# A hybrid SSD and delta-rule layer on one core: the first RMSNorm scaled in place on token rows, its transposes read from PSUM

## The chip, the cores and the metric

The kernel runs on one core of a Trainium2 chip. The time is device microseconds of one execution. A run is one execution; before the change three runs were taken, with a median of 2346.11 us (2344.76 to 2347.41). One more execution was taken by the hardware profiler.

## The reference, cut to what matters

One step of an encoder layer on 336 tokens: 16 learned meta tokens and 256 prompt tokens of one stream, 64 sample tokens of another. `D_MODEL` is 2048. The change lies in the first line of the layer and its first uses:

```python
def _rmsnorm(x, w):
    xf = xf * lax.rsqrt(jnp.mean(xf * xf, axis=-1, keepdims=True) + EPS)
    return (xf * w.astype(jnp.float32)).astype(x.dtype)

u = _rmsnorm(x, norm_mix_w)
z_a, xbc_a, dt_a, qkv_b, z_b, beta_b, a_b, gate_a, gate_b = jnp.split(u @ w_in, SPLIT_IDX, axis=-1)
```

`u @ w_in` feeds a Mamba-2 mixer (causal convolution, chunked scan, gate, norm) and a gated DeltaNet; their outputs go through `w_out`, two sigmoid gates and the residual, then a squared-ReLU MLP, a last residual and a last norm. All is float32.

## The kernel before, in words

**Products.** Every float32 operand of a product is split into a high part of type float32r and a rest (`lo = x - hi`); a product is three matmuls, hi by hi, hi by the rest of the other, rest by hi. Activations lie channel-major: channels on the 128 partitions, the 336 tokens along the free axis. `uh` and `ul` are the two parts of u, 16 tiles of 128 channels each (a *k-tile*).

**Weights.** All weight blocks of the kernel stand in one list (`stream`), 592 pieces of four k-tiles by 256 columns (512 KB). `wload` (line 193) sends piece n through SP's DMA queue into one of three `raw` buffers; `wsplit` (201) lets ScalarE make `hi` and VectorE `lo` (GpSimd for piece 3, line 208). `block` (213) is a generator that runs over the pieces of one block: it loads piece n+3, splits up to piece n+2 (in the first block `hold` keeps it from that, and the start does it by hand), and gives two output tiles `pt` of 128 columns by 336 tokens; each step between two yields is three matmuls.

**The order of the work.** TensorE's instructions keep the order of the program text throughout (line 73). Inside `manual` (343 to 472) all engines and queues do. Outside it, a scheduler places the instructions of the other engines and of the DMA queues by its own estimate of when they are ready; such an instruction may slip in between those of the manual part. `run` (240) weaves the matmuls of a projection with the scan of the group before.

**The start.** x comes as three tiles of 112 token rows: `xs[0]` holds the meta tokens and 96 prompt rows, `xs[1]` 112 prompt rows, `xs[2]` 48 prompt and 64 sample rows. SP's queue carries x0 and x1, then five small loads `prow` (norm weights and convolution biases as rows), then x2, then the first three weight pieces. For each tile `sumsq` (321) forms the sums of squares (ScalarE, VectorE or half by half), `root` (334) the reciprocal root with a power on GpSimd, and `flip` (328) transposes four k-tiles at a time into a PSUM buffer of the pool `scr` (four buffers), from which ScalarE or VectorE copies them to `xT` (16 k-tiles of unscaled x; the residual needs it later, `scratch` writes it to DRAM). The roots stand per token on partitions; to scale channel-major data, `spread_d` (339) puts them on diagonals, a product with ones (`prx`) spreads them over all partitions, and `rbx` is their copy. Then, per k-tile, `u_scale` (380) forms `ut = xT * rbx` on VectorE for even and GpSimd for odd k-tiles, and `u_split` (384) makes `uh` (ScalarE, with the norm weight as scale) and `ul` (VectorE). The loop at 464 emits these four k-tiles ahead of the first block's steps.

**Behind the block.** The last step of the first block is left for `run`. After `manual.close()` come the loads of the convolution weights and states as rows (`cra`, `crb`, `sra`, `srb`, 475 to 486), of `dvec` (488) and `pb` (490 to 493), and of `wt` (503, 504); the rows are turned by TensorE and copied by VectorE (`load_cols`, 306), and `ptok` (505) is the projection of the 64 narrow columns. All these tiles but `dvec` lie in pool `sp`, opened after `xctx.close()` (375), in memory that x held. `tokens` (516) then computes `nega` from `pb` on ScalarE, among others.

Of the kernel before, what the change touches and what calls it, by code (L numbers as in the profile page):

```python
# [21 lines left out]
NT = NMETA + NPR + NSA  # L22
# [20 lines left out]
def tile_hybrid_step(ctx: ExitStack, tc: tile.TileContext, i: dict, o: dict):  # L43
    nc = tc.nc
# [148 lines left out]
    def wload(n):  # L193
        if n >= len(stream) or n in raws:
            return
        raw = wpool.tile([P, 4, 256], F32, tag="raw", name="raw", bufs=3)
        for c0, src in stream[n]:
            nc.sync.dma_start(raw[:, :, c0:c0 + src.shape[1]], src.rearrange("(k p) c -> p k c", p=P))
        raws[n] = raw

    def wsplit(n):
        if n >= len(stream) or n in split:
            return
        wload(n)
        hi = wpool.tile([P, 4, 256], F32R, tag="hi", name="hi", bufs=3)
        act(hi, raws[n])
        lo = wpool.tile([P, 4, 256], F32R, tag="lo", name="lo", bufs=3)
        tt(G if n == 3 else V, lo, raws[n], hi.bitcast(F32), SUB)
        split[n] = hi, lo

    used, hold = [0], [len(stream)]
# [73 lines left out]
        G.memset(t, 0.0)  # L285
    xctx = ExitStack()
    xp = xctx.enter_context(tc.tile_pool(name="xp", bufs=1))
    xs = []
    segs = [[(0, "meta", 0, 16), (16, "pr", 0, 96)], [(0, "pr", 96, 112)], [(0, "pr", 208, 48), (48, "sa", 0, 64)]]
    src = {"meta": i["meta_tokens"], "pr": i["x_prompt"][0], "sa": i["x_sample"][0]}  # L290
    def load_x(n):
        for p0, s, r0, nr in segs[n]:
            nc.sync.dma_start(xs[n][p0:p0 + nr, :], src[s][r0:r0 + nr, :])

    for n in range(3):
        xs.append(xp.tile([112, D], F32, name=f"x{n}"))
# [17 lines left out]
    junk = acc.rearrange("p k n -> p (k n)")[:112, :]
    ssx = sp0.tile([112, 4], F32, name="ssx")
    rsx = sp0.tile([112, 3], F32, name="rsx")
    dgx = sp0.tile([112, 3, 112], F32, name="dgx")
    rbx = sp0.tile([P, NT], F32, name="rbx")
    HD = D // 2

    def sumsq(f, x, d0, n):
        d = junk[:, d0:d0 + x.shape[1]]
        if f is act:
            act(d, x, AF.Square, accum_out=ssx[:, n:n + 1])
        else:
            V.scalar_tensor_tensor(out=d, in0=x, scalar=1.0, in1=x, op0=MUL, op1=MUL, accum_out=ssx[:, n:n + 1])

    def flip(n, k):
        ps = scr("pu").rearrange("p (k t) -> p k t", k=4)[:, :, :112]
        for m in range(4):  # L330
            transp(ps[:, m, :], xs[n][:, (k + m) * P:(k + m + 1) * P])
        return xT[k // 4][:, :, n * 112:(n + 1) * 112], ps

    def root(n):
        r = rsx[:, n:n + 1]
        V.tensor_scalar(out=r, in0=ssx[:, n:n + 1], scalar1=1.0 / D, scalar2=EPS, op0=MUL, op1=ADD)
        tt(G, r, r, nhalf_pow[:112, 0:1], ALU.pow)

    def spread_d(n):
        V.tensor_scalar(out=dgx[:, n, :], in0=ident[:112, :112], scalar1=rsx[:, n:n + 1], scalar2=None, op0=MUL)  # L340

    manual = ExitStack()
    manual.enter_context(tc.manual_schedule())

    pw_ = scr("pwarm")
    for n in range(8):
        mm(pw_[:, :P], ident, ident)
    prx = psb.tile([P, 512], F32, tag="big", name="prx")
    sumsq(act, xs[0], 0, 0)
    for k in range(0, KD, 4):  # L350
        (V.tensor_copy if k < 8 else act)(*flip(0, k))
    root(0)
    sumsq(V, xs[1], D, 1)
    for k in range(0, KD, 4):
        act(*flip(1, k))
    root(1)
    load_cols(par, prow, 73)
    for n in range(3):
        wload(n)
    sumsq(act, xs[2][:, :HD], 0, 2)  # L360
    sumsq(V, xs[2][:, HD:], D, 3)
    tt(V, ssx[:, 2:3], ssx[:, 2:3], ssx[:, 3:4], ADD)
    root(2)
    spread_d(0)
    spread_d(1)
    act(*flip(2, 0))
    late = [flip(2, k) for k in (4, 8, 12)]
    spread_d(2)
    wsplit(0)
    for n in range(3):  # L370
        mm(prx[:, n * 112:(n + 1) * 112], ones[:112, :], dgx[:, n, :])
    act(rbx, prx[:, :NT])
    for a in late:
        act(*a)
    xctx.close()
    sp = start.enter_context(tc.tile_pool(name="sp", bufs=1))

    ut = {}

    def u_scale(k):  # L380
        ut[k] = sp0.tile([P, NT], F32, tag="ut", name="ut", bufs=6)
        tt(G if k % 2 else V, ut[k], xT[k // 4][:, k % 4, :], rbx, MUL)

    def u_split(k):
        t, w = ut.pop(k), par[:, NM + k:NM + k + 1]
        act(uh[:, k, :], t, AF.Copy, scale=w)
        stt(ul[:, k, :], t, w, uh[:, k, :].bitcast(F32), MUL, SUB)

# [68 lines left out]

    main0 = kept(proj_ssd(0), tiles0)  # L460
# [12 lines left out]
    hold[0] = len(stream)

    cra = sp.tile([96, P], F32, name="cra")
    nc.sync.dma_start(cra, i["ssd_conv_w"][0].rearrange("k (t c) -> (k t) c", c=P))
    crb = [sp.tile([96, P], F32, name=f"crb{n}") for n in range(2)]
    crb_src = i["gdn_conv_w"][0].rearrange("k (t c) -> (k t) c", c=P)
    for n in range(2):
        nc.sync.dma_start(crb[n], crb_src[n * 96:(n + 1) * 96, :])  # L480
    sra = sp.tile([72, P], F32, name="sra")
    nc.sync.dma_start(sra, i["state_ssd_conv"][0, 0].rearrange("k (t c) -> (k t) c", c=P))
    srb = [sp.tile([72, P], F32, name=f"srb{n}") for n in range(2)]
    srb_src = i["state_gdn_conv"][0, 0].rearrange("k (t c) -> (k t) c", c=P)
    for n in range(2):
        nc.sync.dma_start(srb[n], srb_src[n * 72:(n + 1) * 72, :])
# [8 lines left out]
    load_cols(cwa.rearrange("p k t -> p (k t)"), cra, 96)  # L495
    load_cols(sta.rearrange("p k t -> p (k t)"), sra, 72)
    for n in range(2):
        load_cols(cwb.rearrange("p k t -> p (k t)")[:, n * 96:(n + 1) * 96], crb[n], 96)
        load_cols(stb.rearrange("p k t -> p (k t)")[:, n * 72:(n + 1) * 72], srb[n], 72)


    wt = sp.tile([P, KD, 64], F32, name="wt")
    nc.sync.dma_start(wt[:, :, 0:32], win[:, C_DT:C_DT + 32].rearrange("(k p) c -> p k c", p=P))
    nc.sync.dma_start(wt[:, :, 32:64], win[:, C_BETA:C_BETA + 32].rearrange("(k p) c -> p k c", p=P))
# [746 lines left out]
```

## Time and profile before

| | us |
|---|---|
| median of three runs | 2346.11 |
| profiled execution | 2343.37 |
| its span from first to last instruction | 2341.5 |
| TensorE busy (matmul) | 2300.9 |
| VectorE busy | 1354.5 |
| ScalarE busy | 1065.4 |
| GpSimd busy | 333.1 |

Times in the profile are microseconds from the start of the span. PE is TensorE's matmul, PEld its weight load, DVE VectorE, ACT ScalarE, POOL GpSimd, SPq the issue of DMAs by SyncE. "L61" is line 61 of the kernel, mostly that of a helper (58 matmul, 61 activation, 64 tensor_tensor, 67 scalar_tensor_tensor, 87 transpose, 309 copy of turned rows). A tile is named without its buffer number. The granted clock (PEclk) is the share of TensorE's full clock.

### The profile page before, as it was taken

The page shows a single profiled execution, that of the slowest core. Times are in us where ns is not written, and L with a number is a line of the kernel's source. Part 1 is how long each engine was busy: PE and PEld are TensorE (multiplying, and loading weights), DVE is VectorE, ACT ScalarE, POOL GpSimd, SP SyncE. Part 2 cuts the span into 40 slices and gives each one's busy share as a digit, 9 for nine tenths or more (in the row PEclk, how much of TensorE's full clock was granted, in tenths as well). Part 3 has the DMA queues.
Part 4 walks back from the last instruction along what each step waited for, and adds up shares of the span by engine and source line. Part 5 has one row for each costly group of instructions (what it writes and reads, how often), then busy time and mean ns, then how long its engine had stood idle before and what let it go on. Part 6 is the DMA issues. An engine that isn't in the chain of part 4 may idle for free.

```text
span 2341.5 us, 40643 instructions
## 1 busy us (share of the span) xinstructions
PE 2300.9 (98%) x16393; PEld 2278.7 (97%) x16393; DVE 1354.5 (58%) x2147; ACT 1065.4 (46%) x1830; POOL 333.1 (14%) x488
## 2 busy tenths in 40 slices
PE   7999999999999999999999999999999999999997
PEld 6999999999999999999999999999999999999997
DVE  6675757575765547668668567444444444444444
ACT  5664545455445545554554445433343244234433
POOL 3142414141121112112212110000000000000000
PEclk9999999999999999999999999999999999999999
DMA  7845454546565555645556644544544454445543
GB/s 193 224 131 161 136 174 126 173 124 179 157 199 172 151 163 137 163 147 144 144 149 161 171 142 145 151 150 151 148 152 153 146 152 153 146 152 151 166 143 117
DMA packets 411046, 362.87 MB, mean 155 GB/s; under 512 B 48329, under 2 KB 407834, under 8 KB 410394
## 3 DMA queue, kind: packets, MB, share of 16 engines
q1 hardware_dynamic: 410746, 360.15, 52.8%
q8 instruction: 128, 2.10, 0.4%
q14 instruction: 60, 0.49, 0.1%
q10 hardware_dynamic: 112, 0.13, 0.0%
HBM read 340.57 MB, written 19.66 MB: 154 GB/s over the span
## 4 chain that ended last, share of the span: by engine, by line
PE 90%; DVE 5%; DMA 2%; ACT 1%; issue 1%; SPq 1%; POOL 0%; ACTq 0%; DVEq 0%
PE pbig L58 84%; DVE lo L64 1%; DMA raw<-in_w_in_dram 1%; PE po L58 1%; DVE pr L64 1%; DVE ubt L858 1%; PE pS L58 0%; DVE c L67 0%; PE pyd L58 0%; PE pw L58 0%; PE pkk L58 0%; PE pqk L58 0%; ACT hi L61 0%; PE ph L58 0%; DMA x<-in_x_sample_dram 0%
## 5 line engine op out<-in xcount | busy, mean ns | idle before, releaser
L64 DVE TENSOR_TENSOR lo<-raw,hi 128x1024 fp32r<-128x1024 f32 x591 | 738.2, 1250 | 711.2 <-ACT hi L61 705.1
L61 ACT ACTIVATE hi<-raw 128x1024 fp32r<-128x1024 f32 x592 | 627.5, 1060 | 890.4 <-PE pbig L58 840.1
L58 PE MATMUL pbig<-uh,hi 128*128 128x320 f32 (+2 forms) x2176 | 689.2, 317 | 4.2 <-ACT uh L61 4.2
L58 PE MATMUL pbig<-ul,hi 128*128 128x320 f32 (+2 forms) x2176 | 682.5, 314 | 4.0 <-DVE ul L67 3.9
L58 PE MATMUL pbig<-uh,lo 128*128 128x320 f32 (+2 forms) x2176 | 681.0, 313 | 0.7 <-DVE lo L64 0.7
L58 PEld LDWEIGHTS pbig<-uh,hi 128*128 128x128 f32 x2176 | 411.3, 189 | 10.0 <-ACT uh L61 4.7
L58 PEld LDWEIGHTS pbig<-ul,hi 128*128 128x128 f32 x2176 | 411.5, 189 | 6.0 <-DVE ul L67 5.8
L58 PEld LDWEIGHTS pbig<-uh,lo 128*128 128x128 f32 x2176 | 411.4, 189 | 1.0 <-DVE lo L64 1.0
L58 PE MATMUL pbig<-hh,hi 128*128 128x320 f32 x1024 | 318.0, 311 | 0.0
L58 PE MATMUL pbig<-hnl,hi 128*128 128x320 f32 x1024 | 317.1, 310 | 0.0
L58 PE MATMUL pbig<-hl,hi 128*128 128x320 f32 x1024 | 316.2, 309 | 0.0
L58 PE MATMUL pbig<-hh,lo 128*128 128x320 f32 x1024 | 316.2, 309 | 0.0
L58 PE MATMUL pbig<-hnh,lo 128*128 128x320 f32 x1024 | 315.8, 308 | 0.0
L58 PE MATMUL pbig<-hnh,hi 128*128 128x320 f32 x1024 | 315.1, 308 | 0.0
L58 PEld LDWEIGHTS pbig<-hnh,lo 128*128 128x128 f32 x1024 | 192.9, 188 | 0.0
L58 PEld LDWEIGHTS pbig<-hl,hi 128*128 128x128 f32 x1024 | 192.6, 188 | 0.0
L58 PEld LDWEIGHTS pbig<-hh,hi 128*128 128x128 f32 x1024 | 192.6, 188 | 0.0
L58 PEld LDWEIGHTS pbig<-hnh,hi 128*128 128x128 f32 x1024 | 192.3, 188 | 0.2
L58 PEld LDWEIGHTS pbig<-hh,lo 128*128 128x128 f32 x1024 | 192.5, 188 | 0.0
L58 PEld LDWEIGHTS pbig<-hnl,hi 128*128 128x128 f32 x1024 | 192.2, 188 | 0.0
L58 PE MATMUL pbig<-yh,hi 128*128 128x320 f32 x512 | 161.2, 315 | 1.1 <-ACT yh L61 1.1
L58 PE MATMUL pbig<-yl,hi 128*128 128x320 f32 x512 | 157.6, 308 | 0.3 <-DVE yl L64 0.3
(303 smaller groups left out, 2418.4 us busy)
## 6 DMA issues: line engine op xcount, KB each, us to landing
raw<-in_w_in_dram SPq DMA_DIRECT2D x256, 512.0 KB, 3.9
raw<-in_w_up_dram SPq DMA_DIRECT2D x128, 512.0 KB, 3.9
raw<-in_w_down_dram SPq DMA_DIRECT2D x128, 512.0 KB, 3.5
raw<-in_w_out_dram SPq DMA_DIRECT2D x64, 512.0 KB, 3.4
raw<-in_w_in_dram SPq DMA_DIRECT2D x32, 256.0 KB, 3.5
em<-rowd SPq DMA_DIRECT2D x8, 512.0 KB, 5.8
u<-uD SPq DMA_DIRECT2D x4, 768.0 KB, 5.5
eab<-rowd SPq DMA_DIRECT2D x8, 336.0 KB
```

Of the source, the lines that this page charges most:

```text
L58: nc.tensor.matmul(out, lhsT=lhsT, rhs=rhs, start=start, stop=stop, **kw)
L61: nc.scalar.activation(out=out, in_=in_, func=func, **kw)
L64: eng.tensor_tensor(out=out, in0=a, in1=b, op=op)
L858: V.tensor_reduce(out=ubt[:NE, j0:, s], in_=v, axis=AX.X, op=ADD)
```

## The change

x is loaded first on SP's queue and `prow` through ScalarE's. The first three weight pieces follow x, then the row loads of the convolution parameters and `wt`, both now in pool `sp0`. After a tile's root is known and its unscaled transposes are taken, `scale` multiplies the token rows in place (ScalarE, VectorE or half by half). `u_tile` then transposes one k-tile of all three tiles into one PSUM buffer, from which `uh` and `ul` are made; three k-tiles are emitted ahead of the block's steps. `warmer` puts matmuls of the identity between. `spread_d`, `prx`, `rbx`, `u_scale` and `ut` go, and piece 3's `lo` is VectorE's. `xctx` closes after the block. The diff, cut to its core:

```diff
-        tt(G if n == 3 else V, lo, raws[n], hi.bitcast(F32), SUB)
+        tt(V, lo, raws[n], hi.bitcast(F32), SUB)
...
-    load_x(0)
-    load_x(1)
+    manual = ExitStack()
+    manual.enter_context(tc.manual_schedule())
+    warm = sp0.tile([P, 1], F32, name="warm")
+    act(warm, ones[:, 0:1], AF.Square)
     prow = sp0.tile([73, P], F32, name="prow")
     for r0, name, nr in ((NM, "norm_mix_w", 16), (SN, "ssd_norm_w", 16), (NP_, "norm_mlp_w", 16), (CB_, "ssd_conv_b", 24), (GN, "gdn_norm_w", 1)):
-        nc.sync.dma_start(prow[r0:r0 + nr, :], i[name][0].rearrange("(t c) -> t c", c=P))
-    load_x(2)
+        nc.scalar.dma_start(prow[r0:r0 + nr, :], i[name][0].rearrange("(t c) -> t c", c=P))
+    for n in range(3):
+        load_x(n)
+    for n in range(3):
+        wload(n)
+
+    turned = []
+    for dst, source, n in ((cwa, i["ssd_conv_w"][0], 96), (sta, i["state_ssd_conv"][0, 0], 72), (cwb, i["gdn_conv_w"][0], 96), (stb, i["state_gdn_conv"][0, 0], 72)):
+        flat = source.rearrange("k (t c) -> (k t) c", c=P)
+        cols = dst.rearrange("p k t -> p (k t)")
+        for r0 in range(0, flat.shape[0], n):
+            row = sp0.tile([96, P], F32, name=f"row{len(turned)}")
+            nc.sync.dma_start(row[:n, :], flat[r0:r0 + n, :])
+            turned.append((cols[:, r0:r0 + n], row, n))
+    wt = sp0.tile([P, KD, 64], F32, name="wt")
+    nc.sync.dma_start(wt[:, :, 0:32], win[:, C_DT:C_DT + 32].rearrange("(k p) c -> p k c", p=P))
+    nc.sync.dma_start(wt[:, :, 32:64], win[:, C_BETA:C_BETA + 32].rearrange("(k p) c -> p k c", p=P))
...
+    def warmer(n):
+        ps = scr("pwarm")
+        for _ in range(n):
+            mm(ps[:, :P], ident, ident)
...
+    def scale(f, n, c0, c1):
+        x, r = xs[n][:, c0:c1], rsx[:, n:n + 1]
+        if f is act:
+            act(x, x, AF.Copy, scale=r)
+        else:
+            V.tensor_scalar(out=x, in0=x, scalar1=r, scalar2=None, op0=MUL)
+
+    def u_tile(k):
+        ps = scr("pu")
+        for n in range(3):
+            transp(ps[:, n * XW:(n + 1) * XW], xs[n][:, k * P:(k + 1) * P])
+        w = par[:, NM + k:NM + k + 1]
+        act(uh[:, k, :], ps[:, :NT], AF.Copy, scale=w)
+        stt(ul[:, k, :], ps[:, :NT], w, uh[:, k, :].bitcast(F32), MUL, SUB)
...
     main0 = kept(proj_ssd(0), tiles0)
     hold[0] = 0
-    for k in range(4):
-        u_scale(k)
+    cp = V.tensor_copy
+    warmer(10)
+    load_cols(par, prow, 73)
+    sumsq(act, xs[0], 0, 0)
+    for k in range(0, KD, 4):
+        flip(0, k, cp if k < 8 else act)
+    root(0)
+    warmer(4)
+    scale(act, 0, 0, D)
+    sumsq(V, xs[1], D, 1)
+    for k in range(0, KD, 4):
+        flip(1, k, act)
+    root(1)
+    warmer(4)
+    scale(V, 1, 0, HD)
+    scale(act, 1, HD, D)
+    sumsq(act, xs[2][:, :HD], 0, 2)
+    sumsq(V, xs[2][:, HD:], D, 3)
+    tt(V, ssx[:, 2:3], ssx[:, 2:3], ssx[:, 3:4], ADD)
+    root(2)
+    for k in range(0, KD, 4):
+        flip(2, k, act)
+    warmer(2)
+    for c in range(2):
+        scale(V, 2, c * 512, (c + 1) * 512)
+    scale(act, 2, HD, D)
+    wsplit(0)
+    LEAD = 3
+    for k in range(LEAD):
+        u_tile(k)
     for k in range(KD):
-        u_split(k)
-        if k + 4 < KD:
-            u_scale(k + 4)
-        if k % 4 == 1 and k < KD - 4:
-            wsplit(k // 4 + 1)
+        if k + LEAD < KD:
+            u_tile(k + LEAD)
         for _ in range(2 if k < KD - 1 else 1):
             next(main0)
+        if k % 4 == 0 and k < KD - 4:
+            wsplit(k // 4 + 1)
     manual.close()
+    xctx.close()
+    sp = start.enter_context(tc.tile_pool(name="sp", bufs=1))
...
+    for t in turned:
+        load_cols(*t)
```

## Rows read from the trace of the kernel before

**Rows 1.** Engine windows: start:end, length, busy us of each engine (instructions), PEclk, DMA share, GB/s

```profile
160.00:2341.50 2181.50, 2158.30 (x15462) 2140.30 (x15460) 1249.01 (x1960) 972.72 (x1677) 285.55 (x406) 1.00 0.52 153
```

**Rows 2.** Timeline of TensorE's matmuls: start, length, instruction, idle time before and what ended it

```profile
21.36 0.42 PE L58 MATMUL pbig<-uh,hi 128*128 128x336 f32 x1 [2.30 <-ACT uh L61]
...
23.11 0.48 PE L58 MATMUL pbig<-uh,lo 128*128 128x336 f32 x1
...
23.39 0.48 PE L58 MATMUL pbig<-ul,hi 128*128 128x336 f32 x1
...
48.40 0.40 PE L58 MATMUL ptok<-uh,wtr 128*128 128x336 f32 x1
...
53.42 0.32 PE L58 MATMUL pbig<-uh,hi 128*128 128x336 f32 x1
```

**Rows 3.** TensorE's waits from 20 to 48.4 us: total us, times, longest

```profile
PE pbig L58 <- ACT uh L61: 4.2, 2, 2.3
PE pbig L58 <- DVE ul L67: 3.9, 4, 2.1
PE pcol L87 <- DVE cwa L309: 1.0, 1, 1.0
```

**Rows 4.** Engine windows inside the start, columns as in rows 1

```profile
18.70:21.36 2.66, 0.36 (x4) 0.18 (x3) 1.71 (x4) 2.27 (x6) 1.74 (x2) 1.00 0.08 1
21.36:25.70 4.34, 3.89 (x14) 3.55 (x14) 4.34 (x5) 4.16 (x7) 3.42 (x3) 0.61 0.26 73
...
42.80:46.00 3.20, 3.20 (x13) 3.20 (x13) 0.81 (x3) 0.08 (x2) 0.00 (x0) 0.50 1.31 181
...
29.00:36.00 7.00, 4.48 (x26) 3.68 (x25) 7.00 (x8) 2.79 (x5) 5.38 (x3) 1.00 0.06 1
```

**Rows 5.** Groups by form on VectorE, 0 to 60 us: count, busy us, mean ns

```profile
L67 DVE SCALAR_TENSOR_TENSOR ul<-ut,par,uh 128x336 fp32r<-128x336 f32 x16 | 12.3, 798 | 3.0 <-ACT uh L61 2.8
...
L64 DVE TENSOR_TENSOR lo<-raw,hi 128x1024 fp32r<-128x1024 f32 x6 | 7.3, 1219 | 3.3 <-ACT hi L61 3.3
```

**Rows 6.** Timeline inside the first block: VectorE, GpSimd, ScalarE and SP

```profile
26.54 1.04 DVE L67 SCALAR_TENSOR_TENSOR ul<-ut,par,uh 128x336 fp32r<-128x336 f32 x2
26.56 0.61 SPq L488 DMA_DIRECT2D dvec<-in_ssd_d_dram  x1
...
33.58 2.61 POOL L64 TENSOR_TENSOR lo<-raw,hi 128x1024 fp32r<-128x1024 f32 x1
...
33.91 3.13 DVE L67 SCALAR_TENSOR_TENSOR ul<-ut,par,uh 128x336 fp32r<-128x336 f32 x2
...
40.76 0.24 ACT L61 ACTIVATE nega<-pb 128x48 f32<-128x48 f32 x1 [7.81 <-DMA pb<-in_gdn_a_log_dram]
```

**Rows 7.** The chain that ended last, at its start: start us, length, what

```profile
1.26 5.52 DMA x<-in_x_prompt_dram
...
6.79 8.07 DMA x<-in_x_sample_dram
```

**Rows 8.** Timeline of x's transposes, copies and Square

```profile
6.91 1.73 PE L87 MATMUL pu<-ident,x 112*128 112x112 f32 x16 [1.64 <-DMA x<-in_x_prompt_dram]
...
10.72 1.85 ACT L61 ACTIVATE xT<-pu 128x448 f32<-128x448 f32 x4 [0.85 <-PE pu L87]
...
14.97 1.06 ACT L61 ACTIVATE acc<-x 112x1024 f32<-112x1024 f32 x1 [2.40 <-DMA x<-in_x_sample_dram]
...
15.01 2.96 PE L87 MATMUL pu<-ident,x 112*128 112x112 f32 x16 [3.03 <-DMA x<-in_x_sample_dram]
```

**Rows 9.** A scaling of 1024 columns on ScalarE, by form, from 2325 us on

```profile
L61 ACT ACTIVATE yt<-yt,frs 128x1024 f32<-128x1024 f32 x2 | 2.2, 1142 | 0.2 <-POOL frs L64 0.2
```

**Rows 10.** Groups by form on ScalarE, 0 to 60 us

```profile
L61 ACT ACTIVATE uh<-ut,par 128x336 fp32r<-128x336 f32 x16 | 8.1, 574 | 3.3 <-DVE ut L64 3.3
L61 ACT ACTIVATE hi<-raw 128x1024 fp32r<-128x1024 f32 x7 | 7.4, 1055 | 0.0
```

**Rows 11.** DMA issues, 0 to 90 us: count, KB each, median us to landing

```profile
wt<-in_w_in_dram SPq DMA_DIRECT2D x2, 256.0 KB, 5.8
```

More of the change, by code (lines that the diff above doesn't have):

```diff
@@ L287, in tile_hybrid_step @@
     xp = xctx.enter_context(tc.tile_pool(name="xp", bufs=1))
-    xs = []
+    XW = NT // 3
     segs = [[(0, "meta", 0, 16), (16, "pr", 0, 96)], [(0, "pr", 96, 112)], [(0, "pr", 208, 48), (48, "sa", 0, 64)]]
     src = {"meta": i["meta_tokens"], "pr": i["x_prompt"][0], "sa": i["x_sample"][0]}
+    xs = [xp.tile([XW, D], F32, name=f"x{n}") for n in range(3)]
+    HD = D // 2
     def load_x(n):
@@ L293, in load_x @@
             nc.sync.dma_start(xs[n][p0:p0 + nr, :], src[s][r0:r0 + nr, :])
-    for n in range(3):
-        xs.append(xp.tile([112, D], F32, name=f"x{n}"))
-    load_x(0)
-    load_x(1)
+    manual = ExitStack()
+    manual.enter_context(tc.manual_schedule())
+    warm = sp0.tile([P, 1], F32, name="warm")
+    act(warm, ones[:, 0:1], AF.Square)
     prow = sp0.tile([73, P], F32, name="prow")
     for r0, name, nr in ((NM, "norm_mix_w", 16), (SN, "ssd_norm_w", 16), (NP_, "norm_mlp_w", 16), (CB_, "ssd_conv_b", 24), (GN, "gdn_norm_w", 1)):
-        nc.sync.dma_start(prow[r0:r0 + nr, :], i[name][0].rearrange("(t c) -> t c", c=P))
-    load_x(2)
-    warm = sp0.tile([P, 1], F32, name="warm")
-    act(warm, ones[:, 0:1], AF.Square)
+        nc.scalar.dma_start(prow[r0:r0 + nr, :], i[name][0].rearrange("(t c) -> t c", c=P))
[14 more added lines that the diff above has]
+    nc.sync.dma_start(wt[:, :, 32:64], win[:, C_BETA:C_BETA + 32].rearrange("(k p) c -> p k c", p=P))
     def load_cols(dst, row, n):
@@ L309, in load_cols @@
         V.tensor_copy(dst, ps[:, :n])
+    def warmer(n):
+        ps = scr("pwarm")
+        for _ in range(n):
+            mm(ps[:, :P], ident, ident)
     xT = [cpool.tile([P, 4, NT], F32, tag=t, name="xT", bufs=b) for t, b in (("q", 2), ("k", 2), ("v", 1))]
     xT.append(sp0.tile([P, 4, NT], F32, name="xT3"))
[L314 to L319, printed above, removed]
+    junk = acc.rearrange("p k n -> p (k n)")[:XW, :]
+    ssx = sp0.tile([XW, 4], F32, name="ssx")
+    rsx = sp0.tile([XW, 3], F32, name="rsx")
     def sumsq(f, x, d0, n):
@@ L326, in sumsq, with flip @@
             V.scalar_tensor_tensor(out=d, in0=x, scalar=1.0, in1=x, op0=MUL, op1=MUL, accum_out=ssx[:, n:n + 1])
-    def flip(n, k):
-        ps = scr("pu").rearrange("p (k t) -> p k t", k=4)[:, :, :112]
+    def flip(n, k, f):
+        ps = scr("pu").rearrange("p (k t) -> p k t", k=4)[:, :, :XW]
         for m in range(4):
             transp(ps[:, m, :], xs[n][:, (k + m) * P:(k + m + 1) * P])
-        return xT[k // 4][:, :, n * 112:(n + 1) * 112], ps
+        f(xT[k // 4][:, :, n * XW:(n + 1) * XW], ps)
     def root(n):
@@ L336, in root @@
         V.tensor_scalar(out=r, in0=ssx[:, n:n + 1], scalar1=1.0 / D, scalar2=EPS, op0=MUL, op1=ADD)
[L337 to L387, printed above, removed]
+        tt(G, r, r, nhalf_pow[:XW, 0:1], ALU.pow)
+    def scale(f, n, c0, c1):
[11 more added lines that the diff above has]
+        stt(ul[:, k, :], ps[:, :NT], w, uh[:, k, :].bitcast(F32), MUL, SUB)
     def ctile(tag, name, bufs):
@@ L461, in tile_hybrid_step @@
     hold[0] = 0
-    for k in range(4):
-        u_scale(k)
-    for k in range(KD):
-        u_split(k)
-        if k + 4 < KD:
-            u_scale(k + 4)
-        if k % 4 == 1 and k < KD - 4:
-            wsplit(k // 4 + 1)
+    cp = V.tensor_copy
[28 more added lines that the diff above has]
+        u_tile(k)
+    for k in range(KD):
+        if k + LEAD < KD:
+            u_tile(k + LEAD)
         for _ in range(2 if k < KD - 1 else 1):
             next(main0)
+        if k % 4 == 0 and k < KD - 4:
+            wsplit(k // 4 + 1)
     manual.close()
+    xctx.close()
+    sp = start.enter_context(tc.tile_pool(name="sp", bufs=1))
     hold[0] = len(stream)
[L475 to L486, printed above, removed]
     for h in range(2):
@@ L493, in tile_hybrid_step @@
     nc.sync.dma_start(pb[:, 1, 32:48], i["gdn_a_log"][0].partition_broadcast(P))
[L495 to L504, printed above, removed]
+    for t in turned:
+        load_cols(*t)
     ptok = psb.tile([P, 512], F32, tag="big", name="ptok")
```

## The prediction

> **What bounds the kernel now.** I read the engine windows first, then the timeline of the stretch that the diff touches, then TensorE's waits. In the windows TensorE is busy for 2158.3 of the 2181.5 us after 160 us, at a granted clock of 1.00 [rows 1]. The order of its instructions is written by hand, and nothing in the diff adds to or takes from the matmuls after the first block. So what the change is worth is how much earlier TensorE gets through the start; the same stream follows. I take the first matmul of `ptok` as the mark, because all that the change moves lies ahead of it: it starts at 48.40 us [rows 2].
>
> Where do those 48.4 us go? The first projection block (31 steps of three matmuls) begins at 21.36 us, behind a 2.3 us wait for `uh` [rows 2]. Inside it TensorE waits for both halves of u: 3.9 us for `ul` and, with the first wait, 4.2 us for `uh`, and behind it 1.0 us for the copy of a turned row [rows 3]. Idle time costs clock too: from 21.36 us the granted clock is 0.61 on average, and from 42.8 us it is 0.50, the lower of the two levels, 1.2 of 2.4 GHz [rows 4]. Two matmuls of a block start 0.28 us apart at the half clock; at the full one `ptok`'s 32 take 5.02 us, 0.157 each [rows 2].
>
> Why is u late? `ul` averages 798 ns on VectorE [rows 5], though two of them take 1.04 us when GpSimd is quiet; two take 3.13 us beside GpSimd's `lo` of 2.61 us [rows 6]. The other wait is ScalarE's: it stands 7.81 us at `nega`, behind the load of `pb`, with the last `uh` queued after it [rows 6].
>
> **The change, part by part.** *The load order.* x is limited by its transfer: the sample rows, the last, have landed at 14.86 us [rows 7]. The five `prow` loads leave SP's queue for ScalarE's; they are 37 KB beside 2.75 MB of x, so I count no earlier landing. The three weight loads are issued right behind x instead of from 10 us; they stood behind x's transfer before as well: nothing for that either.
>
> *The norm in place.* It adds three scalings of x, removes the spread of the roots, `rbx`, the 16 products `ut` (half on VectorE, half on GpSimd) and GpSimd's `lo`, and lets `uh` and `ul` read PSUM. Most of the scaling falls on ScalarE, so I follow its queue. x0 has landed at 6.78 us [rows 7]; its Square, twice the 1.06 us of half a one, lasts to 8.9; two copies of `xT`, half of the 1.85 us for four, to 9.8 [rows 8]; the scaling of 112x2048, twice the 1.14 us of 1024 columns less one fixed cost, about 2.0, to 11.8 [rows 9]; four copies to 13.7; half a scaling to 14.8. That is when x's last rows land, so this queue has no slack. From 14.97: half a Square 1.06, four copies 1.85, half a scaling 1.14, `hi` 1.05, `uh` 0.57 [rows 8 to 10]: 20.6, and the first matmul at 20.8 against 21.36. VectorE's halves run beside it. `lo` (1.22 us [rows 5]) ends at 21.4 and the first `ul` half a microsecond later, so the third matmul starts at 22.0.
>
> *The block.* Each k-tile gives TensorE six matmuls and three transposes, ScalarE one `uh` and a quarter of `hi` (0.57 + 0.26 = 0.8 us), VectorE one `ul` at 0.52 and a quarter of `lo` (0.52 + 0.31 = 0.8 us). TensorE needs 6 x 0.157 plus 3 x 0.107 (sixteen transposes in 1.73 us [rows 8]), 1.26 us. So it becomes the bound of its own block. How fast `ul` is from PSUM is not shown: I bound it by 0.52 and by its mean with GpSimd at work, 0.80, and take 0.52, since GpSimd has no part left in the block; at 0.80 a tile takes VectorE 1.1 us, still under TensorE's 1.26, so both ends give the same sum. After 22.0 us, 91 matmuls and 36 transposes are left: 14.3 + 3.9 = 18.2 us, to 40.2. TensorE again stands almost idle for two microseconds ahead of the block, so I expect one stretch at the half clock like the first of before, about 3.3 us long, which costs half of itself, 1.65 (bounds: none, or two). The block ends at 41.8.
>
> *The parameters turned later.* Six row loads and the two `wt` loads go ahead of the fourth weight load in SP's queue, so `wt` no longer comes last. The six transposes and copies stay behind the block, but VectorE is free by then: 0.8 us in all, without the wait of 1.0. `ptok` starts at 42.6: **48.4 - 42.6 = 5.8 us gained.** GpSimd's `lo`, back on VectorE, costs 1.22 us inside VectorE's slack.
>
> *What is late next.* `pb`, the source of `nega`, lies in memory that x holds to its last transpose, so its load can start only near 38 us, behind the queue that has built up. ScalarE's evacuation of the block and the next `hi` stand behind `nega` if the schedule puts it there: between nothing and 3.6 us (rival 1). I take nothing, because every `uh` is through by then.
>
> **The sum.** The profiled execution took 2343.37 us (2341.5 of span and 1.9 around it), 2.7 under the median of the three runs, 2346.11. Less 5.8 it would be 2337.6; against the median 2340.3. The runs lie within 1.4 us of their median, and about 0.2%, 4.7 us, can be told from no change.
>
> **The rivals.**
> 1. *ScalarE's wait for `pb` moves to the end of the block.* For it: the 7.81 us are there already, and the load now starts later. In the profile that wait cost TensorE 2.0 us of idle time and 3.2 us at half clock from 42.8, so 1.6: 3.6 in all [rows 3, 4, 6]. The gain falls to 2.2: 2343.9, no change that can be told. Against: the next weights are needed only 5 us later, after `ptok`.
> 2. *The fourth weight load is late.* The `dvec` load of 4 KB stalls its queue: behind its second half, issued at 26.56 us, the DMA engines moved 1 GB/s for seven microseconds [rows 4, 6]. In the new queue there is room for it ahead of the fourth weights. The transfers before it end near 24.4 us: 18.7, where the DMA fell idle before [rows 4], and some 5.7 for rows and `wt`, by `wt`'s time to landing [rows 11]. Two halves at 7.5 us, the weights at 1.6, `hi` and `lo`: 43.3, where TensorE wants them at 38.5. With a clock fall of 1.6 that costs 6.4: **2346.7, slower than before by 0.6.** One half alone ends at 35.8 and costs nothing; it decides from a fourth load that lands after 36.2 us. Before, one half went ahead, and the queue had more empty time there.
> 3. *ScalarE is blocked by its own DMA issues.* The sample rows, tenth on SP, were issued only when the second had landed, at 6.78 us [rows 7]: eight may be open. If SP's eight loads are counted first and the limit is common to both queues, ScalarE's fifth `prow` issue waits for x's last rows at 14.9, and TensorE, whose first real work turns `prow`, until some 3 us later. The queue above then runs to 30.6 in place of 20.6: 10 us lost, **2350.3, slower by 4.2.** It decides from a `prow` that lands after 8 us. Against it: counted in the order of the program, `prow` comes first and waits for nothing.
> 4. *The clock stays low through the block*, since 3 of each 9 instructions are transposes. The rows speak against it: x0's transposes ran at 0.107 us, and the sixteen that took 2.96 us came after three microseconds without work [rows 8]. At the half clock the block takes 91 x 0.28 + 36 x 0.185 = 32.2 us after 22.0, 12.3 more than forecast: 2352.6. The Trainium skill ("TensorE: Matmul & The Clock Gate", Part 4) says that a transpose does not count as TensorE work for the clock; that speaks for this rival and against the change. By that rule the short warming matmuls that the change puts between x's transposes are all that holds the clock ahead of the block; the trace, whose fast transposes follow warming matmuls closely, cannot separate the two.
>
> **How the numbers follow.** Forecast 0.55; rival 1 0.20; rival 2 0.10; rival 3 0.09; rival 4 0.03; nothing gained for a reason not seen 0.03. The forecast's own range is 5.8 with 1.65 less or more for the clock and about one for the rest, 2337.6 to 2343; the whole range goes down to 2336.5 (no clock fall, and a run at the low end of the spread) and up to 2348, past rival 2, and leaves out rivals 3 and 4. Faster by over 0.2%: the forecast's part above 4.7 us, about 0.45, and 0.05 for gains past it, 0.50. Slower by over 0.2%, above 2350.8: rival 4, half of rival 3, and rivals 1 and 2 together, 0.11. The rest, 0.39, lies between.
>
> **What would show it.** Right: first matmul of the block near 20.8, no wait for `ul` or `uh` inside it, `ul` near 0.52 us, no GpSimd work between, `ptok` near 42.6. Rival 1: ScalarE's wait at `nega` ahead of `pre` or `hi`. Rival 2: TensorE waits at the fourth chunk, k-tile 12. Rival 3: the first transposes of x start after 8 us. Rival 4: granted clock 0.50 past 30 us. Wrong altogether: `ptok` after 46 us, or a gain at `ptok` that is gone by 160 us.

## The result, and the profile after

The changed kernel takes 2357.53 us (median of four runs, 2355.9 to 2359.05) against 2345.44 for the kernel before in the same session (2342.17 to 2347.41): a ratio of 1.0065, 95% interval [1.0051, 1.0078]. It is slower by 0.65%, where the forecast was 2340.3 and the range ended at 2348.0. The profiled execution has a span of 2357.3 us, 15.8 more than before.

TensorE's waits over the whole execution after the change (what waits, line, for whom: us in total, times, longest) hold two long ones that the kernel before has nowhere in its execution:

```profile
PE pbig L58 <- ACT hi L61: 13.0, 1, 13.0
PE pcol L87 <- DMA prow<-in_gdn_norm_w_dram: 6.4, 1, 6.4
```

The waits for `uh` and `ul`, 8.1 us together in [rows 3], are down to one of 1.4 us for the first `uh`. So the part that the change was made for works, and two other waits took its place. TensorE's timeline shows where:

```profile
11.86 0.35 PE L87 MATMUL pcol<-ident,prow 73*128 73x73 f32 x1 [6.36 <-DMA prow<-in_gdn_norm_w_dram]
12.01 3.20 PE L87 MATMUL pu<-ident,x 112*128 112x112 f32 x16
...
27.21 0.42 PE L58 MATMUL pbig<-uh,hi 128*128 128x336 f32 x1 [1.44 <-ACT uh L61]
...
28.52 0.65 PE L58 MATMUL pbig<-ul,hi 128*128 128x336 f32 x1
...
47.85 1.02 PE L87 MATMUL pcol<-ident,row 96*128 96x96 f32 x6
48.67 0.40 PE L58 MATMUL ptok<-uh,wtr 128*128 128x336 f32 x1
...
54.00 0.32 PE L58 MATMUL pbig<-ul,hi 128*128 128x336 f32 x1
67.33 0.65 PE L58 MATMUL pbig<-uh,hi 128*128 128x336 f32 x1 [13.02 <-ACT hi L61]
```

Read it against [rows 2, 8]. x's first transposes start at 12.01 instead of 6.91, because TensorE first turns `prow`, and `prow` lands only now. The block begins at 27.21, 5.9 us later than before, but takes 20.6 us instead of 25.3, and `ptok` starts 0.3 us later than before. Up to here the change has gained and lost the same. Then TensorE stands 13.0 us for the split of the next weight piece. Take the first matmul of `pcum`, some 25 us of work behind `ptok`, as a second mark; here it is in the kernel after, and then in the kernel before:

```profile
89.10 0.50 PE L58 MATMUL pcum<-la,tri 80*80 80x48 f32 x4
```
```profile
73.30 0.56 PE L58 MATMUL pcum<-la,tri 80*80 80x48 f32 x4 [0.47 <-DVE la L64]
```

The difference there is 15.8 us, the whole difference of the spans. All of the loss lies ahead of 90 us, and 15.5 of it between the two marks: 13.0 of idle time, and the half clock that follows it. In the windows (start:end, length, busy us and instructions of each engine, granted clock, DMA share, GB/s):

```profile
28.00:32.00 4.00, 3.90 (x14) 3.61 (x15) 3.59 (x6) 1.94 (x4) 0.00 (x0) 0.57 0.43 131
32.00:47.85 15.85, 15.85 (x116) 15.68 (x115) 9.49 (x15) 8.68 (x15) 0.00 (x0) 1.00 0.16 33
36.00:48.00 12.00, 12.00 (x89) 11.89 (x88) 7.89 (x13) 6.55 (x12) 0.00 (x0) 1.00 0.05 0
67.30:73.00 5.70, 5.33 (x19) 4.81 (x20) 5.23 (x9) 3.17 (x6) 0.74 (x2) 0.51 1.00 265
```

The block is cold (near the half clock, 0.57) until 32 us and then at 1.00 to its end. Behind the wait 5.7 us run at 0.51: half of that, 2.8 us, is lost again. And in the twelve microseconds from 36 to 48 the DMA engines move next to nothing, at a share of 0.05. Who stands in front? ScalarE's timeline, then SP's (start, length of the issue):

```profile
48.05 0.51 ACT L61 ACTIVATE pre<-pbig 128x272 f32<-128x272 f32 x2 [2.49 <-PE pbig L58]
63.10 0.24 ACT L61 ACTIVATE nega<-pb 128x48 f32<-128x48 f32 x1 [14.54 <-DMA pb<-in_gdn_a_log_dram]
...
66.24 1.04 ACT L61 ACTIVATE hi<-raw 128x1024 fp32r<-128x1024 f32 x1
```
```profile
28.02 3.40 SPq L198 DMA_DIRECT2D raw<-in_w_in_dram  x2
31.47 1.42 SPq L489 DMA_DIRECT2D dvec<-in_ssd_d_dram  x2
...
39.93 16.37 SPq L994 DMA_DIRECT2D xTd<-xT  x7
57.28 0.38 SPq L198 DMA_DIRECT2D raw<-in_w_in_dram  x1
57.71 0.50 SPq L994 DMA_DIRECT2D xTd<-xT  x1
58.31 0.38 SPq L491 DMA_DIRECT2D pb<-in_ssd_dt_bias_dram  x1
```

This is the wait of [rows 6] again, 14.5 us in place of 7.8, and now with `hi` behind it on ScalarE. `nega` needs `pb`; `pb` lies in memory that x held, and its loads are issued only at 58.3. But x is free much earlier, its last transposes start at 44.3. In between, SP needs 16.4 us to issue seven `xTd`, 8.6 of them for a single one. I read this as waiting for room in a queue whose head does not move: the two halves of `dvec`, which now stand side by side and take 21.1 us from issue to landing. The DMA view of 36 to 48 us (queue: packets, MB, share of 16 engines; then issues) shows what moves:

```profile
q1 hardware_dynamic: 1290, 0.01, 4.7%
issues: line engine op xcount, KB each, median us to landing
xTd<-xT SPq DMA_DIRECT2D x4, 160.0 KB, 17.2
```

That is 1290 packets in 12 us that add up to 0.01 MB. `dvec` is loaded element by element (64x16x1, twice, 4 bytes each), at 108 packets per microsecond, and everything else in the queue waits.

### The profile page after: what moved, and what is told of

The parts are those of the page before. It is cut to its first block, busy times and chain, and to the rows that moved or that the text cites. A ratio compares the mean times of both kernels' runs of the same rounds, so it can differ in the third digit from the quotient of the medians.

```text
span 2357.3 us, 40767 instructions
## 1 busy us (share of the span) xinstructions
PE 2308.6 (98%) x16459; PEld 2287.2 (97%) x16459; DVE 1346.9 (57%) x2140; ACT 1067.0 (45%) x1832; POOL 320.8 (14%) x479
## 4 chain that ended last, share of the span: by engine, by line
PE 91%; DVE 4%; DMA 2%; ACT 1%; issue 1%; POOL 0%; SPq 0%; ACTq 0%; DVEq 0%; POOLq 0%
PE pbig L58 84%; DVE lo L64 1%; DMA raw<-in_w_in_dram 1%; PE po L58 1%; DVE c L67 1%; DVE pr L64 1%; DVE ubt L853 1%; PE pS L58 0%; ACT hi L61 0%; PE pw L58 0%; PE pkk L58 0%; PE pqk L58 0%; PE ph L58 0%; PE pyd L58 0%; DMA prow<-in_gdn_norm_w_dram 0%
## 5 line engine op out<-in xcount | busy, mean ns | idle before, releaser
L58 PE MATMUL pbig<-uh,hi 128*128 128x320 f32 (+2 forms) x2176 | 690.9, 317 | 14.5 <-ACT hi L61 13.0
```

## The experiments

The theory after this reading: the norm in place does what was forecast, and the loss is two matters of the loads, `pb` behind `dvec` (some 16 us) and `prow` late (some 6 us). Eleven kernels tested it. Their ratios are to the kernel before, run beside them on the same chip (medians of 2340.7 to 2341.6 us, 19 to 27 runs of 2338 to 2348; the changed kernel's own was against 2345.4, so ratios are compared and not times). The marks are from the profiled execution of each, in us: the block's first matmul, the first of `ptok`, the first of `pcum`.

| kernel | ratio to before, 95% interval | median | block | ptok | pcum |
|---|---|---|---|---|---|
| before | 1 | 2341 | 21.36 | 48.40 | 73.30 |
| after | 1.0065 [1.0051, 1.0078] | 2357.5 | 27.21 | 48.67 | 89.10 |
| pb_early | 1.0056 [1.0044, 1.0069] | 2354.7 | 27.45 | 48.75 | 84.60 |
| dvec_rows | 1.0001 [0.9992, 1.0010] | 2342.2 | 27.19 | 47.13 | 74.13 |
| par_late | 1.0037 [1.0024, 1.0049] | 2349.4 | 20.87 | 43.34 | 82.59 |
| all3 | 0.9983 [0.9974, 0.9992] | 2337.3 | 20.91 | 43.53 | 68.06 |
| b_both | 0.9980 [0.9971, 0.9989] | 2336.8 | 22.30 | 44.40 | 68.68 |
| all3_nowarm | 0.9990 [0.9981, 0.9999] | 2338.6 | 21.68 | 44.26 | 69.29 |
| prow_sp | 0.9982 [0.9973, 0.9991] | 2337.4 | 22.41 | 43.56 | 68.29 |
| dvec_actq | 1.0039 [1.0025, 1.0052] | 2350.1 | 33.70 | 53.63 | 79.25 |
| all3_warm | 0.9967 [0.9955, 0.9980] | 2334.7 | 20.77 | 40.65 | 64.96 |
| b_warm | 0.9976 [0.9966, 0.9987] | 2335.7 | 21.41 | 43.55 | 67.85 |
| all3_gplo | 0.9993 [0.9984, 1.0002] | 2339.2 | 20.91 | 43.52 | 70.06 |

### pb loaded early

```diff
+    pb = sp0.tile([P, 2, 48], F32, name="pb")
+    nc.sync.dma_start(pb[:, 0, 0:32], i["ssd_dt_bias"][0].partition_broadcast(P))
...
-    pb = sp.tile([P, 2, 48], F32, name="pb")
-    nc.sync.dma_start(pb[:, 0, 0:32], i["ssd_dt_bias"][0].partition_broadcast(P))
...
```

All four loads move from behind the block to behind those of `wt`, into a pool of their own.

> The four loads of pb stand ahead of dvec, with memory of their own, so nega no longer waits for x's memory nor for what stands behind dvec. Theory (the changed kernel loses 13.0 us of TensorE idle time plus about 3 us of half clock at nega, behind a load queue that dvec stalls): nega runs before 30 us, the 13.0 us wait for hi after ptok shrinks, the first matmul of the block stays at 27.2 us, and the time falls by 9 to 16 us, to 2341 to 2349 us; the fifth weight load still stands behind dvec, which may keep a few us of the wait. Rival A (the weight load itself, not nega, is what comes last: hi of the fifth chunk would be as late without nega): the wait for hi stays at 10 us or more and the time within 4 us of the changed kernel, 2354 to 2358 us. Rival B (the loss is not at this wait but in the way u is made): ptok later than 50 us or no change of the time.

Measured: 2354.7 us, 1.0056. By the ratios that is 2 us under the changed kernel, where the theory had 9 to 16, and the two intervals overlap. `nega` now runs at 45.54 without a wait, and the fifth weight piece is split at 52.08, in time. But the wait comes again three pieces on, at the eighth. ScalarE's timeline, then TensorE's, then SP's:

```profile
45.54 0.23 ACT L61 ACTIVATE nega<-pb 128x48 f32<-128x48 f32 x1
...
52.08 1.04 ACT L61 ACTIVATE hi<-raw 128x1024 fp32r<-128x1024 f32 x1
...
57.96 1.06 ACT L61 ACTIVATE hi<-raw 128x1024 fp32r<-128x1024 f32 x1 [1.51 <-DMA raw<-in_w_in_dram]
71.65 1.06 ACT L61 ACTIVATE hi<-raw 128x1024 fp32r<-128x1024 f32 x1 [12.62 <-DMA raw<-in_w_in_dram]
```
```profile
72.75 0.65 PE L58 MATMUL pbig<-uh,hi 128*128 128x336 f32 x1 [6.91 <-ACT hi L61]
```
```profile
53.75 5.50 SPq L994 DMA_DIRECT2D xTd<-xT  x10
...
64.14 5.46 SPq L198 DMA_DIRECT2D raw<-in_w_in_dram  x5
```

TensorE's wait for `hi` falls from 13.0 to 6.9 us, and half clock follows it as before (0.50 from 72 to 78 us). The eighth piece is issued only at 64.14, behind ten `xTd` and eight writes of zeros; those stand in the queue behind `dvec`, for whose landing SP waits 7.1 us. From 54 to 64 us nothing is stalled any more: the engines move 386 GB/s. So Rival A has the time but not the piece: its fifth is in time, and its wait of 10 us or more is 6.9. In both kernels what comes last stands in the queue behind what `dvec` held up. `nega` was only the first to be late, and the theory's price for it alone was too high: the marks say 4.5 us at `pcum`, the ratios 2.

### dvec as whole rows

```diff
+    dvr = sp0.tile([P, 32], F32, name="dvr")
+    nc.sync.dma_start(dvr, i["ssd_d"][0].partition_broadcast(P))
     for h in range(2):
-        nc.sync.dma_start(dvec[h * 64:(h + 1) * 64, :], i["ssd_d"][0].rearrange("(t h) -> h t", h=2)[h].partition_broadcast(64))
+        G.tensor_copy(dvec[h * 64:(h + 1) * 64, :], dvr.rearrange("p (t h) -> p h t", h=2)[h * 64:(h + 1) * 64, h, :])
```

> dvec comes as one load of whole 128-byte rows, spread by two GpSimd copies, in place of two loads of 4-byte elements; pb stays where it is, behind x's memory. Theory (the two dvec loads stall SP's queue for about 16 us, and pb stands behind them): the xTd load before pb takes under 6 us in place of 16.4, the pb loads are issued once x's memory is free at about 45 us and nega runs at 47 to 52 us, the wait for hi shrinks from 13.0 to under 4 us, and the time falls by 9 to 15 us, to 2342 to 2348 us. Rival (the stall belongs to x's memory alone, dvec only happens to be there): nega still after 58 us and the time within 3 us of the changed kernel.

Measured: 2342.2 us, 1.0001: 15 us come back (1.0065 - 1.0001 of 2341) from two loads of 4 KB, although what replaces them brings 16 KB. SP's queue shows it:

```profile
31.45 0.50 SPq L489 DMA_DIRECT2D dvr<-in_ssd_d_dram  x1
32.00 1.93 SPq L996 DMA_DIRECT2D xTd<-xT  x4
...
36.62 3.70 SPq L996 DMA_DIRECT2D xTd<-xT  x7
...
43.24 0.33 SPq L493 DMA_DIRECT2D pb<-in_ssd_dt_bias_dram  x1
```

Seven `xTd` are issued in 3.7 us instead of 16.4, `pb` at 43.2, as soon as x's memory is free. `nega` still waits, for 2.6 us until 49.6, and TensorE for `hi` 1.1 us. The theory holds; the rival, that x's memory is the cause, falls. (Of the 15.0 us at `pcum`, 1.5 lie ahead of `ptok`: in this execution the block ran at a granted clock of 1.00 from 28 us on, for which the edit gives no reason.)

### prow turned later

```diff
     warmer(10)
-    load_cols(par, prow, 73)
...
     root(1)
+    load_cols(par, prow, 73)
```

> The turning of prow, TensorE's first real work, moves behind the transposes of x1, where the kernel before has it; nothing else changes. Theory: x0's transposes start at about 7 us in place of 12.0, the first matmul of the block at 21 to 23 us in place of 27.2, and ptok near 43 us in place of 48.7. As the wait for pb is set by SP's queue (dvec, xTd) and not by TensorE, it moves only as far as x's memory comes free earlier: the time falls by 0 to 6 us, to 2351 to 2358 us, with the wait for hi growing by what ptok gains if dvec alone sets it. Rival (prow late costs nothing, ScalarE's queue of copies and scalings sets the block's start anyway): the first matmul of the block stays within 1 us of 27.2.

Measured: 2349.4 us. The block starts at 20.87 and `ptok` at 43.34, 5.3 us earlier. The wait for `hi` stays at 12.1 us, because `dvec` and all behind it were issued earlier by about as much (25.1 instead of 31.5). The saving, 1.0065 - 1.0037 = 0.28% or 6.6 us, is a little past what was expected, and the rival falls.

### The three together

> The three edits together. Theory: the 13.0 us wait and its half clock go and the start comes 5 us earlier: ptok near 43 us, no wait over 2 us after it, the time 2335 to 2340 us, 5 to 10 us under the kernel before. Rival (half clock in the block, or GpSimd and VectorE work that meets in it, takes part of that back): ptok near 43 us but the time above 2342 us.

Measured: 2337.3 us, 0.9983 [0.9974, 0.9992], 4 us under the kernel before and about 19 under the change. TensorE's timeline:

```profile
20.91 0.42 PE L58 MATMUL pbig<-uh,hi 128*128 128x336 f32 x1 [1.44 <-ACT uh L61]
21.73 0.65 PE L58 MATMUL pbig<-uh,lo 128*128 128x336 f32 x1 [0.41 <-DVE lo L64]
22.21 0.65 PE L58 MATMUL pbig<-ul,hi 128*128 128x336 f32 x1
```

The prediction had put these at 20.8 and 22.0, and `ptok`, which stands at 43.53, at 42.6. So this is the kernel that the prediction described.

### The kernel before with the same loads

`pb` early and `dvec` as rows, in the kernel before; no norm in place.

> The kernel before with the two load edits of the changed kernel's best version so far (pb loaded early into memory of its own, dvec as whole rows), without the norm in place: what the norm in place is worth by itself is the distance from here to all3, which stands at 2337.3 us. Theory (the prediction's price of ScalarE's 7.8 us stand at nega in the kernel before, 2.0 us idle and 1.6 us of half clock, is right, and the rest of the way to all3 is the norm in place): ptok at 44.5 to 46 us, 2337.5 to 2339.5 us, so the norm in place itself is worth 1 to 2.5 us. Rival A (the loads are worth nothing to the kernel before): ptok at 48 us, the time within 1.5 us of before, and the norm in place is worth 4 to 5 us. Rival B (the gain of all3 is all from the loads): time at or under that of all3.

Measured: 2336.8 us, 0.9980: rival B in the time, since it is level with all3. Its `ptok` at 44.40 is 4.0 us earlier than before, close to the 3.6 that the prediction had worked out for ScalarE's stand at `nega` and a little better than the theory; all3 is 0.9 ahead of it there. So of the 4.9 us that all3 gains at `ptok`, 4.0 are the loads', which the kernel before could have had without the change. What is left over for the norm in place, 0.9 us, is less than these runs can tell.

### No warming matmuls between x's transposes

```diff
     root(0)
-    warmer(4)
...
     root(1)
...
-    warmer(4)
...
-    warmer(2)
```

> all3 without the ten warming matmuls that the change puts between x's transposes (the ten at the start stay). Theory (transposes of x hold the clock as matmuls do, or the clock of the start hides behind ScalarE's queue): the transposes of x1 and x2 still at 0.107 us each, the first matmul of the block and ptok within 1 us of all3, the time within 2 us of its 2337.3. Rival (transposes do not count for the clock): granted clock 0.50 from about 10 us to past the block's start, x's transposes 0.185 us each, ptok 1.5 to 4 us later than all3 and the time 2339 to 2341 us.

Measured: 2338.6 us, `ptok` 0.7 us later than all3: the theory's times, but not by its first reason. The transposes do run at the half clock for most of the time, as the rival said. x1's sixteen take 3.22 us, and x2's sixteen with the first twelve for the block stand in this row of the timeline, with the granted clock in windows inside it:

```profile
15.41 4.43 PE L87 MATMUL pu<-ident,x 112*128 112x112 f32 x28 [1.12 <-DMA x<-in_x_sample_dram]
```
```profile
15.40:17.00 1.60, 1.59 (x9) 1.60 (x10) 1.35 (x3) 1.60 (x4) 0.00 (x0) 0.50 1.10 349
...
18.50:19.00 0.50, 0.50 (x6) 0.50 (x5) 0.25 (x1) 0.33 (x1) 0.00 (x0) 0.88 1.09 326
19.00:19.80 0.80, 0.80 (x9) 0.62 (x7) 0.00 (x0) 0.80 (x2) 0.00 (x0) 1.00 1.17 261
```

Twenty-eight transposes without a gap, nothing else, and the clock rises from 0.50 to 1.00 under them. What had lowered it is not shown apart: TensorE had stood idle for 1.8 us ahead of x0's transposes, and the clock fell while those ran, from 0.98 (7.9 to 8.4 us) to 0.50 (8.4 to 8.9). That cost little, since the block starts only 0.8 us later (21.68 and 20.91); I take it that ScalarE's queue of copies and scalings sets that start. The Trainium skill ("TensorE: Matmul & The Clock Gate", Part 4) has it that a transpose does not count as TensorE's work for the clock; here, in float32, the clock rose under transposes alone, and the measurement decides.

### prow first on SP's queue

```diff
-        nc.scalar.dma_start(prow[r0:r0 + nr, :], i[name][0].rearrange("(t c) -> t c", c=P))
+        nc.sync.dma_start(prow[r0:r0 + nr, :], i[name][0].rearrange("(t c) -> t c", c=P))
```

in all3, with `prow` turned ahead of x0's transposes, as in the change.

> all3 with prow's five loads first on SP's queue, ahead of x's later rows' packets, and turned first as in the changed kernel, in place of ScalarE's queue and a late turn. Theory (prow came at 11.8 us because its 134 small packets alternate on the engines with x's large ones of another queue, not because a 37 KB load is slow): prow's last load lands before 6 us, TensorE's wait for it goes, x0's transposes start at 7 to 9 us, x lands at most 2.5 us later (five issues), ptok within 2 us of all3 (43.5 us), the time 2336 to 2340. Rival (small loads of one 512-byte row per packet are slow by themselves): prow still after 9 us, ptok 3 us or more later than all3, time over 2340.

Measured: 2337.4 us, level with all3. TensorE turns `prow` at 5.99 us and without a wait; x0's transposes start at 9.02, 2.1 us later than [rows 8], which is what the five issues and their packets cost x. So the same five loads are through by 6 us when they stand ahead of x in its queue, and at 11.8 us when they stand in another queue beside it. In the changed kernel the DMA view of 0 to 14 us has

```profile
q1 hardware_dynamic: 467, 2.80, 85.3%
q10 hardware_dynamic: 134, 0.04, 1.6%
```

134 packets of `prow` (q10) beside 467 of 6 KB on average (q1). Cut into stretches of four microseconds, they come as 32, 45 and 57, beside 74, 147 and 136 large ones: they move at the pace of the others. That they take turns with x's packets is argued from these counts and from the two landings. The Trainium skill ("DMA: Bandwidth & Descriptors", Queues, rings and completion order) says that each engine goes round its queues packet by packet. The trace agrees in kind and not in the proportion: one small packet goes with two or three large ones, not with one.

### dvec's elements on ScalarE's queue

```diff
+    for h in range(2):
+        nc.scalar.dma_start(dvec[h * 64:(h + 1) * 64, :], i["ssd_d"][0].rearrange("(t h) -> h t", h=2)[h].partition_broadcast(64))
```

in all3, behind `prow`, and `dvr` with its copies gone.

> all3 with dvec again as two loads of 4-byte elements, but on ScalarE's queue behind prow, while x and the first weights move on SP's. Theory A (a load of 4-byte elements stalls only the queue that it stands in): x's last rows land near 15 us as before, the weights and pb as in all3, ptok within 1 us of 43.5, the time within 2 us of all3's 2337.3. Theory B (it stalls the DMA engines themselves, whatever queue it is in): x's rows or the weights land 8 to 16 us later, ptok after 50 us, the time 2345 us or more.

Measured: 2350.1 us, by the ratios 13 over all3 (1.0039 and 0.9983). Theory B, in the main. TensorE's waits, and the DMA view of 14 to 20 us:

```profile
PE pu L87 <- DMA x<-in_x_sample_dram: 8.0, 1, 8.0
PE pu L87 <- DMA x<-in_x_prompt_dram: 5.7, 2, 4.5
```
```profile
DMA  0000000000000000000000000000848599968593
...
q1 hardware_dynamic: 52, 0.39, 27.0%
q10 hardware_dynamic: 568, 0.00, 4.7%
```

From 14.0 to 18.2 us q10 works through `dvec`'s elements and q1 moves nothing (the zeros of the forty slices), though x's last rows were issued at 7.65; TensorE gets them at 27.43. So the elements hold up the engines and not only their own queue, and another queue is no way out. They do not do it all the time: from 8 to 14 us q1 moves 0.89 MB at a share of 44.3% beside 529 packets of q10, and why it stands still in one stretch and not in another is not shown. Nor is all of x's delay theirs: SP issues x's last rows 3.4 us later than in all3 (4.21), after waits of 2.8 and 2.5 us for `prow`. The Trainium skill ("DMA: Bandwidth & Descriptors", Rules for kernel authors) says that a last dimension that is not contiguous becomes one descriptor per element and should be rearranged. The packet counts agree (568 in 6 us, and 0.00 MB); what it costs the other queue is measured here.

### Warming matmuls ahead of the block

```diff
     for k in range(LEAD):
         u_tile(k)
+    warmer(6)
```

> all3 with six warming matmuls behind the first three u tiles, in TensorE's idle time ahead of the block's first matmul. In all3 the block starts at 20.9 us and runs at the half clock from 22 to 28 us, which by the rows costs about 3 us where the prediction had put 1.65. Theory (the clock falls because TensorE is nearly idle for two microseconds ahead of the block; filling them keeps it at the full clock): k-tiles at 1.23 us from the start, ptok at 40.5 to 41.5 us in place of 43.5, the time 2 to 3 us under all3, 2334 to 2336 us. Rival (the clock falls in any case, or ul and lo, not the clock, set the pace of the first tiles): the half clock is still there, or it goes and ptok moves by less than 1 us; the time within 1 us of all3.

Measured: 2334.7 us, 0.9967 [0.9955, 0.9980], the lowest ratio of all, though its interval overlaps those of all3, b_both, prow_sp and b_warm. In all3 the block runs cold, with six warming matmuls it does not; first a window of all3, then two of this kernel:

```profile
22.00:28.00 6.00, 6.00 (x23) 5.68 (x24) 3.85 (x7) 2.18 (x4) 0.00 (x0) 0.50 0.53 79
```
```profile
20.00:22.00 2.00, 1.53 (x9) 0.87 (x8) 1.72 (x3) 2.00 (x6) 0.00 (x0) 1.00 1.19 113
22.00:24.00 2.00, 1.96 (x14) 1.93 (x15) 2.00 (x4) 1.46 (x2) 0.00 (x0) 1.00 0.87 125
```

`ptok` comes at 40.65, 2.9 us earlier: that is what the cold stretch cost, where the prediction had put 1.65. The theory holds, the rival falls.

### The same for the kernel before

Eight warming matmuls behind the first four `u_scale`, in b_both.

> The kernel before with both load edits (b_both) and eight warming matmuls in TensorE's idle time ahead of its block, where it runs at the half clock from 23.3 to 27.2 us. Theory (without the norm in place TensorE waits for ul four times in the block, 3.8 us in all, so the clock gives little back: what is won at the full clock is lost again in the waits): ptok at 43 to 44.4 us in place of 44.4, the time within 1.5 us of b_both, 2335 to 2337 us. So the norm in place is worth its lead over this kernel once both are warm: 2 to 3 us at ptok. Rival (the clock helps both alike): ptok at 42.5 us or less.

Measured: 2335.7 us; `ptok` 0.9 us earlier than in b_both, but so is the block's first matmul (21.41 and 22.30): from there to `ptok` both take 22.1 us. The granted clock is 1.00 from 20 us on, and TensorE's waits take back what that gives:

```profile
PE pbig L58 <- DVE ul L67: 5.1, 5, 2.0
```

against 3.8 us in b_both. With a warm clock the norm in place leads by 2.9 us at `ptok` (40.65 and 43.55), inside what was expected; 0.6 of it is an earlier start of the block. In the time the medians are 1.0 us apart and the intervals overlap, so this lead is shown at the mark and not in the whole.

### GpSimd's lo put back

```diff
-        tt(V, lo, raws[n], hi.bitcast(F32), SUB)
+        tt(G if n == 3 else V, lo, raws[n], hi.bitcast(F32), SUB)
```

> all3 with lo of the fourth weight chunk back on GpSimd, as the kernel before has it. The prediction gave ul 0.52 us with GpSimd quiet and 0.80 beside its work, and counted neither for the end, since TensorE bounds the block. Theory: lo takes about 2.6 us on GpSimd and the ul beside it 0.8 to 1.5 us each; TensorE waits for ul or lo once or twice around k-tile 12, ptok 0 to 1.5 us later than all3, the time within 2 us of its 2337.3. Rival (GpSimd's lo was what made u late in the kernel before): a wait of 2 us or more for ul in the block, ptok 2 us later or more.

Measured: 2339.2 us, 0.9993; `ptok` at 43.52, as in all3. GpSimd's and VectorE's timelines:

```profile
36.34 2.39 POOL L64 TENSOR_TENSOR lo<-raw,hi 128x1024 fp32r<-128x1024 f32 x1 [4.85 <-issue]
```
```profile
36.68 0.57 DVE L67 SCALAR_TENSOR_TENSOR ul<-pu,par,uh 128x336 fp32r<-128x336 f32 x1 [0.81 <-ACT uh L61]
37.19 2.09 DVE L64 TENSOR_TENSOR wtr<-wt,wtr 128x512 fp32r<-128x512 f32 x1
```

The part is without effect on the block, as the prediction had it. (`pcum` comes 2.0 us later, behind VectorE's `la`; whether that goes back to `lo` was not followed, and the intervals overlap.) No `ul` is slow beside GpSimd this time: the one that reads PSUM takes its 0.57 us, and `wtr`, which reads SBUF, 2.09 in place of 0.68. It is one instance of each.

## Why the prediction was wrong

**The norm in place: right.** ScalarE's queue, followed step by step, gave a first matmul at 20.8 us and a third at 22.0; all3 has 20.91 and 22.21. `ul` was taken as 0.52 us and measures 0.56, the mean of sixteen from 0.80 in [rows 5]. TensorE bounds the block at 1.23 us per k-tile (1.26 forecast). The block takes 20.6 us in the changed kernel and 21.8 in all3, where the forecast had 21.0, and the six turned rows 0.8 as forecast. The cold stretch, 1.65 with bounds of none and two of them, measures 2.9.

**"What is late next": the step that failed.** The prediction saw that `pb` could load only once x was released and behind "the queue that has built up", priced it "between nothing and 3.6 us" and took nothing. It measured 13.0 us of idle time and 2.8 of clock. The upper bound was the wait of the kernel before, where the halves of `dvec` stand apart, issued at 11.55 and at 26.56 us [rows 6], while the change puts both in a row, in front of the `xTd` and of `pb`. The number was at hand: rival 2 counts 7.5 us for each half, twice, but asks only whether the fourth weight piece stands behind them, and it does not (both `raw` issues at 28.02 precede `dvec`). The same 15 us were not carried on to `pb` further back in the queue, and to what stands behind `pb` on ScalarE, `hi`. pb_early shows that even this would have been a part only: with `pb` early, the eighth weight piece is late.

**Rival 1** named the right wait at nearly the right place, with a price of 3.6 for 15.8. Its argument against, that the next weights are needed only five microseconds later, is true and far too little cover for sixteen.

**The load order: the second failed step.** "The five `prow` loads leave SP's queue for ScalarE's; they are 37 KB beside 2.75 MB of x, so I count no earlier landing" weighs what x gains. That `prow` itself might land later was considered only in rival 3, by slots for issues. ScalarE's issues were not blocked: the fifth was out at 4.0 us. (It is SP that waits for `prow`, 3.0 and 1.4 us ahead of its weight loads; what that costs was not tested.) The landing at 11.8 us still passed the 8 us that rival 3 named, and cost 6.3 us at the block's start (27.21; 20.87 in par_late), by another mechanism: small packets beside x's large ones in another queue, by the argument under prow_sp. TensorE's queue is in order, and the change had put the turn of `prow` in front of all of x's transposes.

**Rival 4** fell: granted clock 1.00 from 32 us on, with three transposes in nine instructions, and all3_nowarm's transposes raise it alone.

**The size of the gain.** The forecast's 5.8 us at `ptok` is 4.9 in all3. But b_both has 4.0 of them without the norm in place. The prediction counted the end of the old wait for `pb` as the change's gain although nothing in the change removes its cause; it only moves it.

## What to carry to other kernels

When a change moves loads, follow every queue to its end: name for each load what stands in front of it, at measured times, and carry a stall on to the last one behind it and to what is queued behind its reader. A load of single elements can be paid by all that shares the engines: bring whole rows and let an engine spread them. Before a gain is put down to a change of the arithmetic, give the old kernel the same loads.

## What the runs showed that was not expected

- Two loads of 4 KB in single elements of 4 bytes move at 108 packets per microsecond, with a DMA share of 0.05. What stands behind them in their queue waits (after, 36 to 48 us), and for 4.2 us of dvec_actq (14.0 to 18.2) nothing moved in the other queue either.
- 37 KB in 134 packets landed at 6 us ahead of 2.75 MB in the same queue, and at 11.8 us beside them in another.
- Transposes alone took the granted clock from 0.50 to 1.00 (all3_nowarm, 15.4 to 19.8 us).
- Beside GpSimd's `lo`, a VectorE operation that reads PSUM kept its 0.57 us while one that reads SBUF went from 0.68 to 2.09 (one instance each).

What was not followed: why the 2.9 us by which all3_warm leads b_warm at `ptok` are not all seen in the time (both profiled spans are 2333.5 us).
